# Low parts of the weights: a vector subtraction replaced by a second DMA that adds onto the negated rounded weights

## The chip, the cores and the metric

The kernel runs on one core of a Trainium2 chip. The metric is the device time of one execution in microseconds (us); three runs were made of the kernel before. Everything about where time goes comes from one execution taken by the hardware profiler.

## What is computed

Two transformer-like layers over 512 tokens of width 2048, in float32. The first (even) layer runs a gated depthwise convolution of 31 taps beside a block attention of 8 heads; the second (odd) layer runs a sparse latent attention of 16 heads whose keys are picked by an indexer. Cut to its products with weights:

```python
def _even_layer(x, ...):
    z = _rmsnorm(x, norm_g) @ w_in                       # 2048 x 7168
    ya = _conformer_conv(...) * silu(a_gate)             # holds a 1024 x 1024 product
    yb = _moba_attention(q, k, v) * silu(b_gate)
    return concatenate([ya, yb], -1) @ w_out             # 2048 x 2048

def _odd_layer(x, ...):
    z = _rmsnorm(x, norm_g) @ w_in                       # 2048 x 2896
    q = (_rmsnorm(cq, q_norm) @ w_qb)                    # then per head with w_uk, w_iq, w_uv
    return (o * silu(gate)) @ w_out                      # 2048 x 2048

x = x + _even_layer(x, ...)
x = x + _odd_layer(x, ...)
return _rmsnorm(x, final_norm)
```

## The kernel before

Activations lie with features on the 128 partitions and the 512 tokens along a row. Every float32 product is made of three products in the engine's rounded format fp32r: each operand is kept as a high part (rounded) and a low part (what is left), and `mm3` adds high by low (line 81), low by high (line 82) and high by high (line 83) into one PSUM tile.

Weights stream from DRAM in pieces of 128 rows by 512 columns (256 KB). `weights` handles one: SyncE's queue (SP) loads the piece into a raw tile `wr`, ScalarE rounds it into `wh` (line 90), VectorE subtracts `wh` from `wr` into `wl` (line 91, in `split`). One piece feeds four steps of a product over 2048 rows, so 12 matmuls. The tiles take turns in slots: `BUFS` gives `wr` four, `wh` and `wl` three each. `x` is split in the same way (lines 93 and 94).

`gemm` makes one output tile of 128 features by 512 tokens and calls `weights` for each piece. The first two tiles are made together by `gemm_pair`, which takes x as it arrives; there the pieces lie in tiles called `C` (raw), `T` (high) and `pt` (low), and the first pieces are smaller (128 and 384 columns). `final` makes the last three output tiles in halves of the tokens with twelve pieces that lie in `A` and `T`; behind that the output tiles take turns in the slots of `wr`, `wh` and `wl`.

The order on each engine comes from a scheduler that places instructions by priorities: `at(t)` sets the priority of what follows to a time t, and `weights` asks for its piece `LEAD` us ahead of the time at which it is wanted. Within an engine the order is then fixed, and an instruction that waits holds those behind it. POOL (GpSimd) does almost nothing.

The three lines that feed a piece:

```python
self.nc.sync.dma_start(raw[:, :n], dram)
i = nc.scalar.activation(th, src, AF.Copy)
nc.vector.tensor_tensor(tl, src, f32(th), op=OP.subtract)
```

Of the kernel before, what the change touches and what calls it, by code (L numbers as in the profile page):

```python
# [9 lines left out]
AF = mybir.ActivationFunctionType  # L10
OP = mybir.AluOpType
PSUM = bass.MemoryType.PSUM
# [3 lines left out]
T = 512  # L16
# [10 lines left out]
KTOP = 128  # L27
# [15 lines left out]
class Builder:  # L43
# [12 lines left out]

# [1 line left out]
    def at(self, t):  # L58
# [5 lines left out]

    BUFS = dict(A1=16, A2=16, G=8, Y=16, T=8, C=8, tmp=4, p=2, wr=4, wh=3, wl=3, u=2, pt=8, row=2, col=24, m8=6)

# [10 lines left out]

# [1 line left out]
    def mm3(self, ps, lh, ll, rh, rl, start, stop):  # L79
# [6 lines left out]
    def split(self, src, th, tl, scale=None):  # L86
        """th + tl = src (or src * scale, a column), th of 12 bits and tl what is left."""
        nc = self.nc
        if scale is None:
            i = nc.scalar.activation(th, src, AF.Copy)  # L90
            nc.vector.tensor_tensor(tl, src, f32(th), op=OP.subtract)  # L91
        else:
            i = nc.scalar.activation(th, src, AF.Copy, scale=scale)
            nc.vector.scalar_tensor_tensor(tl, src, scale, f32(th), op0=OP.mult, op1=OP.subtract)
        return getattr(i, "ins", i)

    LEAD = 8.0

    def weights(self, dram, t, tags=("wr", "wh", "wl")):
        """A piece [128, n] of a weight matrix as its two parts, wanted at t."""  # L100
        n = dram.shape[-1]
        self.at(t - self.LEAD)
        raw = self.s(tags[0], (P, PIECE))
        wh = self.s(tags[1], (P, PIECE), F32R)
        wl = self.s(tags[2], (P, PIECE), F32R)
        self.nc.sync.dma_start(raw[:, :n], dram)
        self.split(raw[:, :n], wh[:, :n], wl[:, :n])
        return wh, wl
# [3 lines left out]
    def gemm(self, dram, xs, m=P, tag="g", n=T):  # L112
        """PSUM tile [m, n] of dram.T @ x; dram is [128, kc, m] laid out flat, xs the parts of x."""
        nk = len(xs)
        ps = self.psum(tag)
        t0 = self.t
        per = PIECE // P
        cuts = list(range(0, nk, per)) + [nk]
        for k0, k1 in zip(cuts, cuts[1:]):
            nkk = k1 - k0  # L120
            wh, wl = self.weights(dram[:, k0 * m:(k0 + nkk) * m], t0 + self.STEP * k0)
            for k in range(nkk):
                self.at(t0 + self.STEP * (k0 + k))
                xh, xl = xs[k0 + k]
                i = self.mm3(ps[:m, :n], wh[:, k * m:(k + 1) * m], wl[:, k * m:(k + 1) * m], xh, xl,
                         k0 + k == 0, k0 + k == nk - 1)
                if k0 + k == 0:
                    self.marks.append((i.ins.name, t0))
        self.t = t0 + self.STEP * nk
        self.at(self.t)  # L130
        return ps
# [15 lines left out]

# [1 line left out]
    def colsum(self, src, rows=P, m=P):  # L149
# [4 lines left out]
    def inv_rms(self, dst, sq, n, rows=P, t=None, cs=range(NT), gap=1.0):  # L154
        """dst[p, t] = (sum_k sq[k, t] / n + EPS) ** -0.5 on every partition p, with one Newton step,
        for the row chunks cs; sq: the squares, or several to be added.  t: when its turn is, where it
        can wait.  Without dst it stays in the PSUM tile that is returned."""
        nc = self.nc
# [28 lines left out]

# [1 line left out]
    def attention(self, q, k, v, bias, ts, tt, tv, ptag="p"):  # L189
        """q (times -SCALE), k: parts [128 d, 512]; v(j): parts [128 s, 128 d]; bias(c): [128 t, 128 (c + 1)],  # L190
        0 or huge.  Returns PSUM [128 d, 512 t].  ts, tt, tv: when the logits, the transposes and the
        products with v have their turn on the tensor engine."""
        nc = self.nc
        # transposed probabilities: key block j holds rows 128 j .. 511; blocks 1 and 3 share a bank
        px = []
# [36 lines left out]

    # -----------------------------------------------------------------------
    def setup(self):
# [48 lines left out]
    def conv_in(self):  # L283
# [3 lines left out]
        for n in range(NCW):  # L287
            if n == 0:
                # the first two products share the pace at which x arrives
                pg, pv = self.gemm_pair(d["w_in"][NCW], d["w_in"][0])  # L290
                self.at(self.t)
            else:
                pg = self.gemm(d["w_in"][NCW + n], self.xs, tag="x" if n == 1 else "g")
# [63 lines left out]
    def even(self):  # L357
# [44 lines left out]
        for n in range(NCW):  # L402
# [5 lines left out]
            self.ys[n] = (yh, yl)  # L408
        # w_out's rows are laid out with those of the attention's half first
        ys = self.ys[NCW:] + self.ys[:NCW]  # L410
# [24 lines left out]
    def normed(self, zs, n, key, tag):  # L435
        """The parts of rmsnorm(z) * g for the tiles zs."""
        nc = self.nc
# [24 lines left out]
    def odd(self):  # L462
        nc, d = self.nc, self.d
        cq = self.normed([self.scaled(n, "C") for n in range(4)], 512, "q_norm", "G")
        ckv = self.normed([self.scaled(4 + n, "C") for n in range(2)], 256, "kv_norm", "T")
        # indexer keys and weights
        m = DI + HI
# [18 lines left out]
        nc.sync.dma_start(ik[DI:, :], ik[:DI, :])  # L486
        # parts of ik stacked for products of 128 rows: low over high and high over low
        lo, hi = slice(0, DI), slice(DI, P)
# [9 lines left out]
        nc.scalar.activation(zh[hi, :], ik[hi, :], AF.Copy)  # L498
        # gates fill the tensor engine while the indexer scores are formed
        gates = []  # L500
# [12 lines left out]
        for i in range(HI // 2):  # L513
            # the rows before KTOP keep all their keys and need no scores
            ps = self.gemm(d["w_iq"][i], [(a[:, KTOP:], b[:, KTOP:]) for a, b in cq], n=T - KTOP)
# [98 lines left out]
    def final(self):  # L614
        """The last product, with the final norm.  Its last tiles are done for the first half of the
        rows and then for the second, so that half of the output leaves under the second half."""
        nc, d = self.nc, self.d
# [5 lines left out]
        def take(n, x, ps, hs):  # L623
            """Columns hs of tile n are in ps."""
            nc.vector.tensor_tensor(x[:, hs], x[:, hs], ps, op=OP.add)  # L625
# [17 lines left out]
        for i in range(late):  # L643
            for k0 in range(0, KC, PIECE // P):
                n = KC - late + i
                ws.append(self.weights(d["w_out2"][n, :, k0 * P:k0 * P + PIECE],
                                       self.t + 5.2 * i + 0.325 * k0, ("wr",) + (("A2", "A2") if i < 2 else ("T", "T"))))
        # has the table of Sqrt at hand for the end
        warm = self.s("m8", (P, 8))
# [24 lines left out]

# bank and first column of each key block of the transposed probabilities
BLOCK = ((0, 0), (1, 0), (2, 0), (1, 384))
# [81 lines left out]
```

## Time and profile before

| | |
|---|---|
| median of 3 runs | 1553.35 us (1553.13 to 1553.88) |
| span of the profiled execution | 1552.0 us, first to last instruction; its own time is not listed apart from it |
| TensorE (PE) busy | 1531.0 us, 99% of the span |
| VectorE (DVE) busy | 987.0 us, 64% |
| ScalarE (ACT) busy | 658.1 us, 42% |
| GpSimd (POOL) busy | 0.4 us |
| DMA, mean share of 16 engines | 30.2%, 152.00 MB |
| granted TensorE clock, mean | 0.996 |

The median lies 1.35 us above the span. Busy time of TensorE counts overlapping products once; a product of 512 columns is listed with about 0.39 us and they start 0.229 us apart. A share of DMA is that of the time in which the 16 engines have packets; it can read slightly over 1 in a full stretch.

### The profile page before, as it was taken

The page shows a single profiled execution, that of the slowest core. Times are in us where ns is not written, and L with a number is a line of the kernel's source. Part 1 is how long each engine was busy: PE and PEld are TensorE (multiplying, and loading weights), DVE is VectorE, ACT ScalarE, POOL GpSimd, SP SyncE. Part 2 cuts the span into 40 slices and gives each one's busy share as a digit, 9 for nine tenths or more (in the row PEclk, how much of TensorE's full clock was granted, in tenths as well). Part 3 has the DMA queues.
Part 4 walks back from the last instruction along what each step waited for, and adds up shares of the span by engine and source line. Part 5 has one row for each costly group of instructions (what it writes and reads, how often), then busy time and mean ns, then how long its engine had stood idle before and what let it go on. Part 6 is the DMA issues. An engine that isn't in the chain of part 4 may idle for free.

```text
span 1552.0 us, 19982 instructions
## 1 busy us (share of the span) xinstructions
PE 1531.0 (99%) x7272; PEld 1276.3 (82%) x7272; DVE 987.0 (64%) x1933; ACT 658.1 (42%) x1177; POOL 0.4 (0%) x5
## 2 busy tenths in 40 slices
PE   8999999999999999999999999999999999999996
PEld 6888888888888888888888887788888888888886
DVE  7699999964654444464444444556598898843344
ACT  7433333334554343443333333445424666643341
POOL 0000000000000000000000000000000000000000
PEclk9999999999999999999999999999999999999998
DMA  6232222222222222224445332222232111133333
GB/s 222 88 102 96 95 96 95 95 86 83 83 83 88 82 88 86 86 86 136 146 140 150 118 99 80 84 89 89 82 96 88 55 51 53 55 122 116 124 128 109
DMA packets 86323, 153.28 MB, mean 99 GB/s; under 512 B 9488, under 2 KB 14736, under 8 KB 86224
## 3 DMA queue, kind: packets, MB, share of 16 engines
q1 hardware_dynamic: 86224, 152.00, 30.2%
q8 instruction: 57, 0.93, 0.3%
q14 instruction: 42, 0.34, 0.1%
HBM read 143.44 MB, written 8.39 MB: 98 GB/s over the span
## 4 chain that ended last, share of the span: by engine, by line
PE 98%; DVE 1%; ACT 0%; issue 0%; DMA 0%; SPq 0%; DVEq 0%; ACTq 0%
PE psg L81 29%; PE psg L83 29%; PE psg L82 29%; PE psx L215 2%; PE pss L82 1%; PE pss L81 1%; PE pss L83 1%; PE pso L82 1%; PE pso L83 1%; PE pso L81 1%; PE pss L528 0%; PE pss L529 0%; PE psx L83 0%; PE psx L82 0%; PE psx L81 0%; PE pso L182 0%
## 5 line engine op out<-in xcount | busy, mean ns | idle before, releaser
L90 ACT ACTIVATE wh<-wr 128x512 fp32r<-128x512 f32 (+1 forms) x480 | 302.1, 630 | 679.8 <-PE psg L83 556.5
L81 PE MATMUL psg<-A,wh 128*128 128x512 f32 x1472 | 580.6, 395 | 0.3 <-DVE tmp L625 0.2
L91 DVE TENSOR_TENSOR wl<-wr,wh 128x512 fp32r<-128x512 f32 (+1 forms) x480 | 330.7, 690 | 321.7 <-ACT wh L90 318.7
L83 PE MATMUL psg<-A,wh 128*128 128x512 f32 (+1 forms) x1264 | 496.3, 393 | 0.0
L82 PE MATMUL psg<-A,wl 128*128 128x512 f32 (+1 forms) x1264 | 495.6, 392 | 0.0
L81 PEld LDWEIGHTS psg<-A,wh 128*128 128x128 f32 x1472 | 276.0, 187 | 60.7 <-issue 1.5
L83 PEld LDWEIGHTS psg<-A,wh 128*128 128x128 f32 (+1 forms) x1264 | 236.8, 187 | 54.4 <-issue 1.2
L82 PEld LDWEIGHTS psg<-A,wl 128*128 128x128 f32 (+1 forms) x1264 | 236.8, 187 | 52.6 <-issue 1.4
L316 DVE SCALAR_TENSOR_TENSOR C<-u,cst,C 128x512 f32<-128x512 f32 x240 | 169.9, 750 | 0.2
L82 PE MATMUL psg<-Y,wl 128*128 128x512 f32 x336 | 131.7, 392 | 0.0
L83 PE MATMUL psg<-Y,wh 128*128 128x512 f32 x336 | 131.3, 391 | 0.0
L83 PE MATMUL psg<-G,wh 128*128 128x512 f32 (+1 forms) x224 | 85.9, 383 | 0.0
L82 PE MATMUL psg<-G,wl 128*128 128x512 f32 (+1 forms) x224 | 85.5, 382 | 0.0
L83 PEld LDWEIGHTS psg<-Y,wh 128*128 128x128 f32 x336 | 63.1, 188 | 14.1
L82 PEld LDWEIGHTS psg<-Y,wl 128*128 128x128 f32 x336 | 63.1, 188 | 13.1
L81 PE MATMUL psg<-T,wh 128*128 128x512 f32 x160 | 63.1, 394 | 1.1 <-DVE A L91 1.1
L81 PE MATMUL psg<-Y,wh 128*128 128x512 f32 x128 | 50.5, 394 | 0.0
L83 PEld LDWEIGHTS psg<-G,wh 128*128 128x128 f32 x224 | 42.0, 188 | 8.3
L82 PEld LDWEIGHTS psg<-G,wl 128*128 128x128 f32 x224 | 42.1, 188 | 7.7
L91 DVE TENSOR_TENSOR pt<-psx,pt 128x512 fp32r<-128x512 f32 (+1 forms) x72 | 42.2, 596 | 9.6 <-ACT pt L90 9.6
L90 ACT ACTIVATE pt<-psx 128x512 fp32r<-128x512 f32 (+1 forms) x72 | 35.7, 521 | 21.2 <-PE psx L215 21.0
L206 ACT ACTIVATE C<-C,col 128x128 f32<-128x128 f32 (+1 forms) x64 | 35.8, 560 | 15.6 <-DVE col L204 15.2
(231 smaller groups left out, 1781.1 us busy)
## 6 DMA issues: line engine op xcount, KB each, us to landing
wr<-in_w_in SPq DMA_DIRECT2D x304, 256.0 KB, 3.0
wr<-in_w_out SPq DMA_DIRECT2D x128, 256.0 KB, 3.0
wr<-in_w_qk SPq DMA_DIRECT2D x32, 256.0 KB, 2.5
Y<-in_xT SPq DMA_DIRECT2D x16, 256.0 KB, 6.1
wr<-in_w_pw SPq DMA_DIRECT2D x16, 256.0 KB, 2.8
tmp<-in_xT SPq DMA_DIRECT2D x16, 256.0 KB, 3.2
x<-tmp SPq DMA_DIRECT2D x16, 256.0 KB, 2.0
tmp<-x SPq DMA_DIRECT2D x16, 256.0 KB, 3.3
```

The source lines that it names most:

```text
L81: i = mm(ps, lh, rl, start=start, stop=False)
L82: mm(ps, ll, rh, start=False, stop=False)
L83: mm(ps, lh, rh, start=False, stop=stop)
L90: i = nc.scalar.activation(th, src, AF.Copy)
L91: nc.vector.tensor_tensor(tl, src, f32(th), op=OP.subtract)
L206: nc.scalar.activation(p[:, :w], p[:, :w], AF.Exp, bias=mn, scale=-1.0, accum_out=sm)
L215: nc.tensor.transpose(px[b][:, o:o + P], p[:, j * P:(j + 1) * P], self.ident)
L316: nc.vector.scalar_tensor_tensor(y, u[:, i:i + T], self.c("w_dw", n * TAPS + i), y, op0=OP.mult, op1=OP.add)
```

## The change

In `weights` the low part is no longer made by VectorE. ScalarE copies the raw piece twice, once rounded into `wh` and once rounded and negated into `wl`, and a second DMA of the same piece from DRAM, issued from POOL's queue, adds the weights onto `wl` (weights minus rounded weights). The slots go from four to two for `wr` and from three to four for `wh` and `wl`, and `LEAD` from 8 to 11. `split` itself stays for activations. Comment lines fall away.

```diff
-    BUFS = dict(A1=16, A2=16, G=8, Y=16, T=8, C=8, tmp=4, p=2, wr=4, wh=3, wl=3, u=2, pt=8, row=2, col=24, m8=6)
+    BUFS = dict(A1=16, A2=16, G=8, Y=16, T=8, C=8, tmp=4, p=2, wr=2, wh=4, wl=4, u=2, pt=8, row=2, col=24, m8=6)
...
-    LEAD = 8.0
+    LEAD = 11.0
...
         self.nc.sync.dma_start(raw[:, :n], dram)
-        self.split(raw[:, :n], wh[:, :n], wl[:, :n])
+
+        self.nc.scalar.activation(wh[:, :n], raw[:, :n], AF.Copy)
+        self.nc.scalar.activation(wl[:, :n], raw[:, :n], AF.Copy, scale=-1.0)
+        self.nc.gpsimd.dma_start(wl[:, :n], dram, accum_op=OP.add)
         return wh, wl
```

ScalarE at the start of the program, before the change. `Y` is a column block of x as loaded, `A` its parts; `C` are raw pieces of weights and `T` their high parts:

```order
L93 ACTIVATE A_4_80<-Y_78,xg 128x512
L90 ACTIVATE T_245<-C_244 128x128
L90 ACTIVATE T_251<-C_250 128x128
L93 ACTIVATE A_7_86<-Y_84,xg 128x512
L90 ACTIVATE T_263<-C_262 128x384
L90 ACTIVATE T_269<-C_268 128x384
L93 ACTIVATE A_10_92<-Y_90,xg 128x512
L93 ACTIVATE A_13_98<-Y_96,xg 128x512
L90 ACTIVATE T_293<-C_292 128x512
L93 ACTIVATE A_16_104<-Y_102,xg 128x512
```

The same place after the change, where lines 108 and 109 are the two copies and `pt` takes the negated one:

```order
L108 ACTIVATE T_245<-C_244 128x128
L109 ACTIVATE pt_246<-C_244 128x128
L108 ACTIVATE T_252<-C_251 128x128
L109 ACTIVATE pt_253<-C_251 128x128
L93 ACTIVATE A_4_80<-Y_78,xg 128x512
L108 ACTIVATE T_265<-C_264 128x384
L109 ACTIVATE pt_266<-C_264 128x384
L108 ACTIVATE T_272<-C_271 128x384
L109 ACTIVATE pt_273<-C_271 128x384
L93 ACTIVATE A_7_86<-Y_84,xg 128x512
L108 ACTIVATE T_297<-C_296 128x512
L109 ACTIVATE pt_298<-C_296 128x512
```

Each piece now takes two places in ScalarE's queue, and both pieces of a pair stand ahead of the next block of x.

TensorE in the last part of the pair, before the change: `psg` and `pss` are the two output tiles of the pair, `A_41` to `A_50` the low parts of the last four blocks of x, and behind them begins the next tile, `psx`:

```order
L81 MATMUL psg_242<-A_47_165,T_365 128x512
L82 MATMUL psg_242<-A_46_164,pt_366 128x512
L83 MATMUL psg_242<-A_46_164,T_365 128x512
L81 MATMUL pss_243<-A_47_165,T_371 128x512
L82 MATMUL pss_243<-A_46_164,pt_372 128x512
L83 MATMUL pss_243<-A_46_164,T_371 128x512
L81 MATMUL psg_242<-A_50_171,T_365 128x512
L82 MATMUL psg_242<-A_49_170,pt_366 128x512
L83 MATMUL psg_242<-A_49_170,T_365 128x512
L81 MATMUL pss_243<-A_50_171,T_371 128x512
```

The same place after the change:

```order
L81 MATMUL psg_242<-A_50_171,T_373 128x512
L82 MATMUL psg_242<-A_49_170,pt_374 128x512
L83 MATMUL psg_242<-A_49_170,T_373 128x512
L82 MATMUL pss_243<-A_40_152,pt_381 128x512
L83 MATMUL pss_243<-A_40_152,T_380 128x512
L81 MATMUL pss_243<-A_44_159,T_380 128x512
L82 MATMUL pss_243<-A_43_158,pt_381 128x512
L83 MATMUL pss_243<-A_43_158,T_380 128x512
L81 MATMUL pss_243<-A_47_165,T_380 128x512
L82 MATMUL pss_243<-A_46_164,pt_381 128x512
L83 MATMUL pss_243<-A_46_164,T_380 128x512
L81 MATMUL pss_243<-A_50_171,T_380 128x512
```

The two tiles no longer alternate by block of x: four blocks go into `psg`, then the same four into `pss`. From the first product with the 13th block (`A_41`) up to where `psx` has TensorE for itself there are 36 products, one of them of `psx`; from the first with the last block (`A_50`) there are 14.

ScalarE beside the softmax of an attention head of the even layer (line 206 before, 209 after, is the exponential), before the change:

```order
L90 ACTIVATE wh_2675<-wr_2674 128x512
L90 ACTIVATE wh_2693<-wr_2692 128x512
L206 ACT_TABLE_LOAD
L206 ACTIVATE p_2596,col_2598<-p_2596,col_2597 128x128
L206 ACTIVATE p_2611,col_2613<-p_2611,col_2612 128x256
L90 ACTIVATE wh_2711<-wr_2710 128x512
```

The same head after the change:

```order
L109 ACTIVATE wl_2805<-wr_2803 128x512
L108 ACTIVATE wh_2804<-wr_2803 128x512
L209 ACT_TABLE_LOAD
L209 ACTIVATE p_2706,col_2708<-p_2706,col_2707 128x128
L209 ACTIVATE p_2721,col_2723<-p_2721,col_2722 128x256
L109 ACTIVATE wl_2824<-wr_2822 128x512
L108 ACTIVATE wh_2823<-wr_2822 128x512
```

The table load and the two exponentials stand between two pieces as before; the negated copy stands ahead of the rounded one.

## Rows read from the trace of the kernel before

**Rows 1.** Page, span and part 1: busy us (share of the span) xinstructions.
```profile
span 1552.0 us, 19982 instructions
PE 1531.0 (99%) x7272; PEld 1276.3 (82%) x7272; DVE 987.0 (64%) x1933; ACT 658.1 (42%) x1177; POOL 0.4 (0%) x5
```

**Rows 2.** Page, the chain that ended last, by engine.
```profile
PE 98%; DVE 1%; ACT 0%; issue 0%; DMA 0%; SPq 0%; DVEq 0%; ACTq 0%
```

**Rows 3.** Busy time by stretch: us, engines, PEclk, DMA share, GB/s.
```profile
39.00:1536.00 1497.00, 1495.22 (x7122) 1247.61 (x7121) 950.60 (x1861) 628.26 (x1126) 0.00 (x0) 1.00 0.30 95
```

**Rows 4.** What TensorE waited for: us in total, times, longest.
```profile
PE psg L81 <- DVE A L94: 6.8, 1, 6.8
```

**Rows 5.** Page, costliest groups: busy us, mean ns, idle before and its releaser.
```profile
L90 ACT ACTIVATE wh<-wr 128x512 fp32r<-128x512 f32 (+1 forms) x480 | 302.1, 630 | 679.8 <-PE psg L83 556.5
...
L91 DVE TENSOR_TENSOR wl<-wr,wh 128x512 fp32r<-128x512 f32 (+1 forms) x480 | 330.7, 690 | 321.7 <-ACT wh L90 318.7
...
L206 ACT ACTIVATE C<-C,col 128x128 f32<-128x128 f32 (+1 forms) x64 | 35.8, 560 | 15.6 <-DVE col L204 15.2
```

**Rows 6.** Timeline of one piece: start us, us, engine, line.
```profile
299.66 0.39 PE L83 MATMUL psg<-A,wh 128*128 128x512 f32 x1
...
301.17 0.33 SPq L106 DMA_DIRECT2D wr<-in_w_in  x1
...
302.41 0.39 PE L83 MATMUL psg<-A,wh 128*128 128x512 f32 x1
```

**Rows 7.** DMA from 100 to 300 us: queue share; issues, KB, us to landing.
```profile
q1 hardware_dynamic: 10444, 19.02, 28.7%
...
wr<-in_w_in SPq DMA_DIRECT2D x73, 256.0 KB, 3.0
```

**Rows 8.** The same from 700 to 870 us, the even layer's output product.
```profile
q1 hardware_dynamic: 13070, 23.79, 46.0%
...
wr<-in_w_out SPq DMA_DIRECT2D x62, 256.0 KB, 3.2
```

**Rows 9.** The same from 0 to 25 us.
```profile
Y<-in_xT SPq DMA_DIRECT2D x16, 256.0 KB, 6.1
```

**Rows 10.** Busy time by stretch of the start; last two: DMA share, GB/s.
```profile
10.00:12.00 2.00, 2.00 (x8) 1.63 (x8) 1.71 (x3) 1.99 (x4) 0.00 (x0) 1.00 1.05 394
...
22.00:24.00 2.00, 2.00 (x10) 1.63 (x10) 1.56 (x3) 1.60 (x4) 0.00 (x0) 1.00 1.07 406
```

**Rows 11.** Timeline of ScalarE at the start.
```profile
3.84 1.28 ACT L93 ACT_TABLE_LOAD   x1 [3.84 <-DMA xg<-in_xg]
5.13 0.72 ACT L93 ACTIVATE A<-Y,xg 128x512 fp32r<-128x512 f32 x1
5.76 0.49 ACT L90 ACTIVATE T<-C 128x128 fp32r<-128x128 f32 x2
...
9.33 0.52 ACT L90 ACTIVATE T<-C 128x384 fp32r<-128x384 f32 x1 [1.84 <-DMA C<-in_w_in]
...
13.20 2.02 ACT L93 ACTIVATE A<-Y,xg 128x512 fp32r<-128x512 f32 x3
...
23.35 1.37 ACT L93 ACTIVATE A<-Y,xg 128x512 fp32r<-128x512 f32 x2 [0.40 <-DMA Y<-in_xT]
```

**Rows 12.** Timeline of the start: TensorE, VectorE, and ScalarE behind the pair.
```profile
7.77 0.63 PE L82 MATMUL psg<-A,pt 128*128 128x512 f32 x1
...
12.69 0.75 DVE L94 SCALAR_TENSOR_TENSOR A<-Y,xg,A 128x512 fp32r<-128x512 f32 x1
...
27.23 1.66 ACT L90 ACTIVATE wh<-wr 128x512 fp32r<-128x512 f32 x3
...
30.99 0.39 PE L81 MATMUL psx<-A,wh 128*128 128x512 f32 x1
```

**Rows 13.** The end: one output tile on VectorE; landing of the stores.
```profile
1542.31 0.75 DVE L671 TENSOR_TENSOR wr<-G,pso 128x256 f32<-128x256 f32 x2 [1.38 <-PE pso L182]
...
outT<-wr SPq DMA_DIRECT2D x6, 256.0 KB, 2.8
```

## The prediction

> **What bounds the kernel now.** I read the page's busy shares first, then the chain that ended last, then what TensorE waited for, and then two stretches closely: the start and an ordinary stretch in the middle. The reader should see one engine only. TensorE is busy 1531.0 of 1552.0 us [rows 1], the chain is TensorE for 98% [rows 2], and of the 1497 us between 39 and 1536 us it is idle for 1.8 [rows 3]. What is left outside lies at the two ends: TensorE's only long wait, 6.8 us before the first product [rows 4], and the last 10 us, in which the output tiles are scaled and stored [rows 13]. VectorE, whose subtraction the change takes away, is busy 64% and ScalarE 42%, and neither holds TensorE anywhere in the middle. So a subtraction that goes can give nothing back there; what matters is whether the new way of making a low part is ever late.
>
> How late it may be is read from the slots. A piece of weights feeds 12 products, and the products stand 2.75 us apart per piece (299.66 to 302.41) [rows 6]. ScalarE's rounding of a piece waits for TensorE to give a slot back (556.5 of the 679.8 us that it idles ahead of those instructions) [rows 5]: it runs as early as the slots let it, and the rest of the chain behind it has time to spare.
>
> **The change part by part.** *Removed:* 480 subtractions of 690 ns from VectorE, 331 us [rows 5], and 22 more like them in the first pair of products and the last three. They lay beside TensorE's work; worth 0 on the path.
>
> *Added on ScalarE:* 502 negated copies. One of 128x512 takes 630 ns as the rounding does [rows 5], so some 310 us: ScalarE goes from 658 to about 970 us, 62% of the span. In the middle that is 1.26 of each 2.75 us, beside TensorE; cost 0 unless something else queues behind it (below).
>
> *Added DMAs:* 502 more transfers of up to 256 KB, behind the negated copy, from POOL's queue. The trace of before has no accumulating transfer and none from POOL. Bounds of its landing: not less than a plain load of the same piece, 3.0 us [rows 7], and for the upper end 6.1 us, what a load takes when the engines are full [rows 9]. An accumulating piece also reads SBUF; the nearest row is the plain load, so I take 3.0 plus the 0.8 us for which a piece holds the engines (28.7% of 2.75 us [rows 7]) = 3.8 us, and keep 3.0 and 6.1. With four slots a piece comes round every 11.0 us; TensorE holds it 2.75, ScalarE needs 1.26, so the transfer may take 7.0 us. Both ends fit. Where an attention head's work stands in ScalarE's queue ahead of a weight piece (a table load of 1.28 us [rows 11] and two exponentials of 0.56 [rows 5] at the place that the order shows), 4.6 us are left: 3.8 fits, 6.1 is 1.5 us late. Over 24 heads that is 0 to 36 us; I take 0.2 a head, an estimate, 5 us.
>
> The Trainium skill ("DMA: Bandwidth & Descriptors", Anatomy of one DMA) gives a transfer issued from GpSimd 2.0 us plus its bytes at 436 GB/s, so an estimate of 2.6 us for a piece. The rows have 3.0 us for a piece from SP's queue, and no run here yet shows one from POOL's. By the page the steady part would cost 0, too.
>
> *Moved: the raw slots.* They go from four to two, and a raw slot is given back only after both copies. Its loop is the landing, two copies (1.26) and SP's issue (0.33 [rows 6]); two slots allow 5.5 us, so the landing may take 3.9 us. It takes 3.0 [rows 7], and 3.2 in the stretch of the output product, where a load and a store of x lie beside [rows 8]. The negated copy that frees the slot also starts the accumulating transfer, so the two now meet on the engines. The lower bound is 3.0; the upper 4.6 is 3.0 plus twice 0.8, if the accumulating piece counts double and lies wholly ahead. At 4.6 a piece comes each 3.1 us instead of 2.75: 0.35 x 440 = 150 us. The nearest row is the stretch with other transfers beside, 3.2, which is hidden: 0, and 150 kept as the upper end.
>
> *Moved: the start.* Here three chains run side by side, and each slips.
> ScalarE: the order shows both copies of two pieces ahead of each few columns of x. Up to the split of the 13th column it now has a table load that ends at 5.1 us, 13 splits at 0.72 (9.4), four copies of 0.25, four of 0.52 and twelve of 0.63 (10.6 instead of 5.3) [rows 11]: 25.1 us, with VectorE's part of 0.75 25.9. From there TensorE's order has 36 products to go at 0.229 (2.75 / 12): the first product behind the pair stands at 34.1 us instead of 30.99 [rows 12], +3. Where copies overlap, as three did in 1.66 us [rows 12] and three splits in 2.02 [rows 11], the chain is 1.9 us shorter: +1.
> The DMA engines: from 10 to 24 us they are full, at about 0.38 MB/us [rows 10]. Eight of the ten accumulating pieces, 1.6 MB, come ahead of the last x: 4.1 us, or 8.3 if each counts double. The last x was split from 23.35 on [rows 11]; behind it must come 0.72, 0.75 and 14 products (3.2), so 2.9 us of the 7.6 up to 30.99 are spare: +1 to +5.
> The first low part: ready at 5.6 us (table load, two copies) plus a landing of 3.0 to 6.1, 8.6 to 11.7, where TensorE took its third product at 7.77 [rows 12]: +1 to +4. Products of that first stretch are listed with 0.63 us where later ones have 0.39 [rows 12], though the granted clock is shown as 1.00, the upper level; that stretch will come later as a whole.
> If they lay wholly side by side the slip would be the largest of them, 1 to 5; if the first two followed on the third, up to 9. I take +5. Then ScalarE squares x between the next pieces, whose accumulated parts have no lead yet: +2, an estimate (a landing of 3.8 against a lead of some 2 us, once).
>
> *The end.* The output tiles take turns in `wr`, `wh`, `wl`; with two `wr` the third waits for the first's store, which lands 2.8 us after its issue, and it comes six tiles of up to 0.75 behind the first, some 4 us [rows 13]: 0, at most 1.
>
> **Sum.** 1552.0 + 5 + 2 (start) + 5 (heads) + 0 (raw loop) + 0 (end) = 1564 us of span. The profile lists the span alone for its execution; the median of the runs is 1.35 above it, so 1565.4. I say **1566 us**.
>
> **The rivals.**
> 1. *The raw loop binds at times* (landing between 3.9 and 4.6 us). For it: two slots, and both transfers start at the same copy. Against: 3.2 us where other transfers lie beside. Up to 1566 + 150; I take half, 1640.
> 2. *An accumulating packet costs the engines twice a plain one.* The plain pieces take 28.7% of the engines [rows 7], the accumulating ones 57%; together 86% in the ordinary stretches, and 46.0 + 57 = 103% in the output product [rows 8], which is past full. There a landing of 6.1 us gives a piece each (6.1 + 1.59) / 2 = 3.85 us, +1.1 over 128 pieces = 141; elsewhere a landing half way between 3.0 and 6.1 gives 3.07, +0.32 over 300 pieces = 96. That is 1566 + 237 = 1803 us. For it: it reads two operands for each one written; against: no row shows that reading is the engine's limit. The Trainium skill ("Collectives: The Full Stack", The bandwidth ceiling) states it as the rule: an adding transfer has two source reads on the same ring and runs at half the rate of a copy, 32.35 against 62.28 GB/s. No run here shows it so far.
> 3. *Not slower.* The start's work fits into what is idle there. The mechanism: ScalarE's copies overlap (0.55 each) and the accumulating transfers queue behind the loads of x, whose last is still split at 23 us. Then the ScalarE chain gives +1, the first low part +1, and the rest 0: 1554 to 1556. It decides when the slip of the first product behind the pair is under 3 us. For it: the 2.9 us to spare behind the last x; against: both engines would have to be without a pause from 4 us on.
> 4. *Faster.* VectorE, freed of 331 us, would have to end the waits in the middle; those come to 1.8 us [rows 3], so at best 1551.5, and only with no loss at the start.
>
> **How the numbers follow.** The forecast (start slips, the rest is hidden but for small stalls; own range 1557 to 1585) 0.50; rival 1, 0.22; rival 2, 0.15; rival 3, 0.10; rival 4, 0.03. The measurement tells about 0.2%, 3.1 us, from no change. Slower by more than that: 0.50 + 0.22 + 0.15 = 0.87; within 0.10; faster 0.03. The range reaches from 1555, which takes half of rival 3, to 1720, the upper end of rival 1: 0.50 + 0.22 + 0.05, and the lower part of rival 2, about 0.8.
>
> **What would show it.** Right: 502 transfers in POOL's queue landing in 3 to 5 us, VectorE's busy time down by some 335 us and ScalarE's up by some 310; the first product into `psx` at 34 to 38 us; TensorE idle below 10 us from 45 to 1536 us. The raw loop: landings of `wr` over 3.9 us, and TensorE waiting at line 81 for ScalarE's `wh`. The double price: DMA shares near 0.85 in the ordinary stretches, TensorE waiting at line 82 for `wl`. The prediction is wrong if the accumulating transfer lands later than 7 us in steady state, since then every piece waits for it; or if TensorE, broken by many short waits, is granted less clock, which no stretch of before shows.

## The result and the profile after

The changed kernel takes 1643.9 us (median of four runs, 1638.24 to 1646.28) where the kernel before, on the same chip, takes 1553.62 (1553.13 to 1554.69): a ratio of 1.0575, 95% interval 1.0558 to 1.0591, so 90 us slower. The profiled execution is the quickest of its four, 1638.24 us with a span of 1636.5, 84.5 more than the span of [rows 1]; the ledger below is made in spans.

The page of the changed kernel: span, busy times, the chain that ended last, the two DMA queues (q0 is POOL's, q1 is SP's; packets, MB, share of 16 engines), and the issues of weights (KB each, us to landing).

```profile
span 1636.5 us, 21088 instructions
...
PE 1564.8 (96%) x7272; PEld 1274.6 (78%) x7272; DVE 677.9 (41%) x1431; ACT 906.0 (55%) x1679; POOL 435.6 (27%) x507
...
q0 software_dynamic: 72288, 130.71, 45.9%
q1 hardware_dynamic: 86224, 152.00, 33.8%
...
issue 43%; PE 30%; POOL 16%; DMA 7%; ACT 2%; DVE 1%; SPq 0%; POOLq 0%; ACTq 0%; DVEq 0%
...
wr<-in_w_in SPq DMA_DIRECT2D x304, 256.0 KB, 4.0
wl<-in_w_in POOLq DMA_DIRECT2D x304, 256.0 KB, 5.2
wr<-in_w_out SPq DMA_DIRECT2D x128, 256.0 KB, 4.7
wl<-in_w_out POOLq DMA_DIRECT2D x116, 256.0 KB, 5.8
```

VectorE lost 309 us of work and ScalarE gained 248, as the change asks. TensorE has the same 7272 products, but it no longer makes up the chain: 30% of it instead of 98 [rows 2]. A plain load of a piece, 3.0 to 3.2 us before [rows 7, 8], now lands in 4.0 to 4.7, and the accumulating transfers take 5.2 to 5.8.

The waits of the changed kernel (engine, tile and line, what it waited for: us in total, times, longest):

```profile
ACT wl L109 <- DMA wr<-in_w_in: 242.4, 147, 3.8
ACT wl L109 <- DMA wr<-in_w_out: 160.5, 90, 5.1
ACT wl L109 <- PE psg L82: 158.5, 126, 4.2
```

Before, ScalarE's first operation on a piece waited for TensorE to give a slot back (556.5 us, [rows 5]); now it waits in 237 cases for the raw piece itself. That is the sign of a raw loop that is too short. Beside it, TensorE's own waits look small:

```profile
PE psg L82 <- DMA wl<-in_w_out: 23.3, 19, 3.8
...
PE psg L82 <- DMA wl<-in_w_in: 5.1, 13, 0.7
...
PE psx L81 <- ACT wh L108: 3.5, 1, 3.5
```

The first two name the accumulated part, the last link of the chain, not the link that is short. Whoever reads only this view would blame the accumulating transfer alone; it is what lengthens the landings (run 2), but with more raw slots it costs little (run 5). The view also shows only a part of the loss. TensorE's idle time grew from 21.0 to 71.7 us (span less busy time), and its listed busy time from 1531.0 to 1564.8 us for the same 7272 products, together the 84.5 us. The weight loads of line 82 wait 65.0 us for `wl` (38.4 for `w_out` and 26.6 for `w_in`) where the products wait 28.4: a gap of a few tenths of a microsecond vanishes under products listed with 0.39 us. A lower granted clock adds some, see below.

Where the 84.5 us lie is read from four lines of VectorE that run once per output tile: the convolution's gate, a tile of each attention head of the even layer, and the two residual additions. Of before (times are the start of the first and of the last):

```profile
L303 DVE SCALAR_TENSOR_TENSOR u<-tmp,cst,tmp x8: 717/747/749, 58.2 to 265.6; 128x512 f32<-128x512 f32 x8
L368 DVE SCALAR_TENSOR_TENSOR tmp<-psg,r x8: 680/692/693, 285.7 to 633.9; 128x512 f32<-128x512 f32 x8
L419 DVE TENSOR_TENSOR tmp<-tmp,psg x16: 686/686/686, 727.3 to 892.3; 128x512 f32<-128x512 f32 x16
L625 DVE TENSOR_TENSOR tmp<-tmp,psg x19: 420/687/689, 1380.0 to 1537.4; 128x512 f32<-128x512 f32 x13, 128x256 f32<-128x256 f32 x6
```

The same four of the changed kernel, whose lines stand three further down:

```profile
L306 DVE SCALAR_TENSOR_TENSOR u<-tmp,cst,tmp x8: 718/750/753, 72.1 to 290.1; 128x512 f32<-128x512 f32 x8
L371 DVE SCALAR_TENSOR_TENSOR tmp<-psg,r x8: 679/692/693, 312.7 to 662.1; 128x512 f32<-128x512 f32 x8
L422 DVE TENSOR_TENSOR tmp<-tmp,psg x16: 686/690/692, 755.6 to 950.5; 128x512 f32<-128x512 f32 x16
L628 DVE TENSOR_TENSOR tmp<-tmp,psg x19: 410/687/690, 1446.6 to 1621.6; 128x512 f32<-128x512 f32 x13, 128x256 f32<-128x256 f32 x6
```

The differences of neighbouring marks make a ledger by stage; the same marks were read in every experiment (us of the profiled execution; the loss is against before):

| stage | before | changed | loss | four raw slots | three raw slots, in order |
|---|---|---|---|---|---|
| start, to the first gate | 58.2 | 72.1 | 13.9 | 73.1 | 68.8 |
| convolution, to the first L368 | 227.5 | 240.6 | 13.1 | 229.2 | 229.1 |
| even attention, to the first L419 | 441.6 | 442.9 | 1.3 | 442.0 | 444.1 |
| output product 1, L419 first to last | 165.0 | 194.9 | 29.9 | 166.3 | 170.4 |
| odd layer, to the first L625 | 487.7 | 496.1 | 8.4 | 488.3 | 488.2 |
| output product 2, L625 first to last | 157.4 | 175.0 | 17.6 | 164.3 | 166.2 |
| end | 14.6 | 14.9 | 0.3 | 15.0 | 14.7 |
| span | 1552.0 | 1636.5 | 84.5 | 1578.2 | 1581.5 |

The loss is largest where pieces of weights follow each other with nothing between them, the output products and the convolution, and is nearly nothing in the even attention, where other products stand between (145 pieces in 442.9 us, 3.05 us a piece).

What goes on there shows between 100 and 300 us, first in the DMA view:

```profile
q0 software_dynamic: 9858, 17.97, 50.4%
q1 hardware_dynamic: 9849, 17.92, 35.2%
...
wl<-in_w_in POOLq DMA_DIRECT2D x69, 256.0 KB, 5.4
wr<-in_w_in SPq DMA_DIRECT2D x69, 256.0 KB, 4.9
```

69 pieces in 200 us are 2.90 us a piece, where before 73 came, 2.74 [rows 7]. And in ScalarE's timeline of that stretch (start us, us, engine, line; in brackets the idle time before and what ended it):

```profile
206.11 0.63 ACT L109 ACTIVATE wl<-wr 128x512 fp32r<-128x512 f32 x1 [0.69 <-DMA wr<-in_w_in]
206.65 0.62 ACT L108 ACTIVATE wh<-wr 128x512 fp32r<-128x512 f32 x1
...
208.93 0.63 ACT L109 ACTIVATE wl<-wr 128x512 fp32r<-128x512 f32 x1 [1.66 <-DMA wr<-in_w_in]
```

ScalarE is idle ahead of most pieces (56 waits for raw pieces, 87.9 us in all, between 100 and 300 us) and starts them when the raw piece lands. Read so, the loop of the two raw slots sets the pace; runs 5 and 9 test it.

### The profile page after: what moved, and what is told of

Read it like the earlier page. It is cut to its first block, busy times and chain, and to the rows that moved or that the text cites. A ratio compares the mean times of both kernels' runs of the same rounds, so it can differ in the third digit from the quotient of the medians.

```text
span 1636.5 us, 21088 instructions
## 1 busy us (share of the span) xinstructions
PE 1564.8 (96%) x7272; PEld 1274.6 (78%) x7272; DVE 677.9 (41%) x1431; ACT 906.0 (55%) x1679; POOL 435.6 (27%) x507
## 3 DMA queue, kind: packets, MB, share of 16 engines
q0 software_dynamic: 72288, 130.71, 45.9%
q1 hardware_dynamic: 86224, 152.00, 33.8%
## 4 chain that ended last, share of the span: by engine, by line
issue 43%; PE 30%; POOL 16%; DMA 7%; ACT 2%; DVE 1%; SPq 0%; POOLq 0%; ACTq 0%; DVEq 0%
POOL wl L110 16%; PE psg L81 8%; PE psg L82 8%; PE psg L83 8%; DMA wr<-in_w_out 4%; PE psx L218 1%; ACT wh L108 1%; DMA wr<-in_w_in 1%; PE pss L82 1%; PE pso L82 1%; PE pso L83 1%; PE pss L83 1%; PE pss L81 1%; DMA C<-in_w_in 1%; PE pso L81 1%
## 5 line engine op out<-in xcount | busy, mean ns | idle before, releaser
L109 ACT ACTIVATE wl<-wr 128x512 fp32r<-128x512 f32 (+1 forms) x480 | 302.0, 629 | 609.9 <-DMA wr<-in_w_in 242.4
L82 PE MATMUL psg<-A,wl 128*128 128x512 f32 (+1 forms) x1264 | 502.5, 398 | 5.8 <-DMA wl<-in_w_in 5.1
L110 POOL DMA_DIRECT2D wl<-in_w_in x304 | 263.5, 867 | 666.8 <-ACT wl L109 646.9
L82 PEld LDWEIGHTS psg<-A,wl 128*128 128x128 f32 (+1 forms) x1264 | 236.8, 187 | 77.3 <-DMA wl<-in_w_in 26.6
L108 ACT ACTIVATE wh<-wr 128x512 fp32r<-128x512 f32 (+1 forms) x480 | 295.1, 615 | 2.3 <-DMA wr<-in_w_in 1.3
L319 DVE SCALAR_TENSOR_TENSOR C<-u,cst,C 128x512 f32<-128x512 f32 x240 | 175.5, 750 | 5.7
L110 POOL DMA_DIRECT2D wl<-in_w_out x116 | 100.4, 866 | 276.2 <-ACT wl L109 265.1
L83 PE MATMUL psg<-Y,wh 128*128 128x512 f32 x336 | 131.8, 392 | 0.0
L82 PEld LDWEIGHTS psg<-G,wl 128*128 128x128 f32 x224 | 42.7, 191 | 34.0 <-DMA wl<-in_w_out 26.6
L422 DVE TENSOR_TENSOR tmp<-tmp,psg 128x512 f32<-128x512 f32 x16 | 11.0, 689 | 124.9 <-PE psg L83 124.9
L110 POOL DMA_DIRECT2D wl<-in_w_qk x32 | 27.7, 866 | 120.2 <-ACT wl L109 112.8
```

The source lines that it names most:

```text
L82: mm(ps, ll, rh, start=False, stop=False)
L83: mm(ps, lh, rh, start=False, stop=stop)
L108: self.nc.scalar.activation(wh[:, :n], raw[:, :n], AF.Copy)
L109: self.nc.scalar.activation(wl[:, :n], raw[:, :n], AF.Copy, scale=-1.0)
L110: self.nc.gpsimd.dma_start(wl[:, :n], dram, accum_op=OP.add)
L319: nc.vector.scalar_tensor_tensor(y, u[:, i:i + T], self.c("w_dw", n * TAPS + i), y, op0=OP.mult, op1=OP.add)
```

## The experiments

Ten kernels ran, each timed beside the kernel before on the same chip. The stage times of a run come from its one profiled execution. The diffs are against the changed kernel where nothing else is said. Two theories stood against each other: **A**, the loop of two raw slots is too short for the landings that the second transfer makes longer; **B**, the DMA engines are as good as full (45.9 + 33.8 = 79.7% of the span, 50.4 + 35.2 = 85.6% in the stretch above), and no number of slots helps. Each expectation words them anew for its run.

**Run 1 (e1). Three raw slots (inconclusive).** So that the tiles take no more memory, `wh` gives one up.

```diff
-    BUFS = dict(..., wr=2, wh=4, wl=4, ..., pt=8, ...)
+    BUFS = dict(..., wr=3, wh=3, wl=4, ..., pt=8, ...)
```

> The changed kernel with three raw slots, three for the high parts and four for the low ones (wr 3, wh 3, wl 4 instead of 2, 4, 4). Theory A (the raw loop is the bound: the accumulating transfers push the landing of a raw piece from 3.0 to 4.0 to 5.1 us, over the 3.9 that two slots allow): three slots allow 6.7 us, so the losses of the convolution stretch (13 us) and most of that of the two output products (30 and 18 us) go; 1585 to 1605 us. Theory B (the engines or the landing of the accumulating piece itself are the bound, whatever the slots): 1630 to 1650 us.

Measured: 1640.8 us, 1.0544 (1.0507 to 1.0581). That is what B asks for. But the edit did something else too. The order of ScalarE's instructions, in which `wr` numbers name the raw piece:

```
L109 ACTIVATE wl_1555<-wr_1553 128x512
L108 ACTIVATE wh_1535<-wr_1534 128x512
L109 ACTIVATE wl_1574<-wr_1572 128x512
L108 ACTIVATE wh_1554<-wr_1553 128x512
```

With three `wh` the rounding of a piece stands behind the negation of the next one, so the third raw slot is held until the next piece lands, and is as good as absent: ScalarE still waits 277.7 and 150.1 us for raw pieces of `w_in` and `w_out`. The run can't tell the theories apart; run 9 repeats it without this.

**Run 2 (e2). A plain second load.** The transfer from POOL's queue only copies; the low part then holds the whole weight, which changes the sum but not the work on any other engine.

```diff
-        self.nc.gpsimd.dma_start(wl[:, :n], dram, accum_op=OP.add)
+        self.nc.gpsimd.dma_start(wl[:, :n], dram)
```

> The changed kernel with the second transfer as a plain copy from POOL's queue instead of an addition: same count, bytes from DRAM, queue and waits, but the destination is not read. The low part then holds the whole weight and not what is left of it. Theory A with the price of the addition (an accumulating packet holds the engines longer because it reads twice): POOL's queue falls from 45.9% of the engines to some 30%, a raw piece lands in 3.3 to 3.7 us, 1570 to 1595 us. If it is the second transfer as such (its queue, its issue, a second read of DRAM) and not the addition: 1630 to 1645 us.

Measured: 1587.82 us, 1.0219 (1.0192 to 1.0245), inside the range of A. The landing of a raw piece, expected at 3.3 to 3.7 us, was missed: it stays at 4.0 to 4.3. The page of this kernel:

```profile
q1 hardware_dynamic: 86224, 152.00, 30.6%
q0 software_dynamic: 72288, 130.71, 30.1%
...
wr<-in_w_in SPq DMA_DIRECT2D x304, 256.0 KB, 4.0
wl<-in_w_in POOLq DMA_DIRECT2D x304, 256.0 KB, 4.1
wr<-in_w_out SPq DMA_DIRECT2D x128, 256.0 KB, 4.3
wl<-in_w_out POOLq DMA_DIRECT2D x116, 256.0 KB, 4.4
```

The same bytes on the same queue hold the engines 30.1% instead of 45.9%; per MB that is 3.65 us of all 16 engines (0.301 x 1586.0 / 130.71) against 5.75 (0.459 x 1636.5 / 130.71), 1.57 times. With four raw slots the same comparison gives 1.48 times (48.8% of 1578.2 us in run 5, 33.3% of 1561.0 in run 6). Against the plain loads of before, 3.08 (0.302 x 1552.0 / 152.00), it is 1.86 times. How much of this is two streams in each other's way is not taken apart. So most of the 84.5 us, 50.5 (1636.5 less 1586.0), comes with the adding, and 32 with a second transfer of any kind beside the first (1586.0 less the 1554.0 of run 3).

**Run 3 (e3). No second transfer.** The line of the second DMA is taken out; the low part is then only the negated high one.

```diff
-        self.nc.gpsimd.dma_start(wl[:, :n], dram, accum_op=OP.add)
```

> The changed kernel without the second transfer: both copies stay on ScalarE, the low part stays the negated rounded weight. Theories A and B alike: raw landing back at 3.0 us, the middle and both output products without loss, only the start 1 to 4 us later; 1553 to 1560 us. If ScalarE's doubled copies or the slots are what costs: 1590 us or more.

Measured: 1556.12 us, 1.0010 (1.0001 to 1.0019); span 1554.0, start 60.4, convolution 227.0, output products 165.0 and 157.3. ScalarE's 502 extra copies, the two raw slots and the new order together cost 2 us of span. ScalarE is not the bound, and two raw slots are enough as long as landings stay at 3.0 us.

**Run 4 (e4). Slots and lead alone.** The kernel before with the numbers of the change and the subtraction kept; against the kernel before:

```diff
-    BUFS = dict(..., wr=4, wh=3, wl=3, ...)
+    BUFS = dict(..., wr=2, wh=4, wl=4, ...)
-    LEAD = 8.0
+    LEAD = 11.0
```

> The kernel before (subtraction on VectorE) with the slots and the lead of the changed one: wr 2, wh 4, wl 4, LEAD 11. Theory A and B: a raw piece lands in 3.0 us, under the 3.9 that two slots allow, so within 3 us of the kernel before, 1551 to 1557 us. If two raw slots cost without any accumulating transfer: 1570 us or more.

Measured: 1554.93 us, 1.0001 (0.9992 to 1.0011). The change of slots does harm only together with the second transfer.

**Run 5 (e5). Four raw slots.** Now all three tags keep four, and `pt` gives up two.

```diff
-    BUFS = dict(..., wr=2, wh=4, wl=4, ..., pt=8, ...)
+    BUFS = dict(..., wr=4, wh=4, wl=4, ..., pt=6, ...)
```

> The changed kernel with four raw slots (wr 4, wh 4, wl 4; pt goes from 8 to 6 to make room). In the run with three raw slots and three for the high parts, a rounding stands behind the negation of the next piece in ScalarE's queue, so a raw slot was held one piece longer and that run did not free the loop. Theory A (the raw loop of two slots with landings of 4 to 5 us): four slots allow 9.4 us, so the convolution stretch loses nothing (228 us instead of 241) and the output products lose less; 1595 to 1615 us. Theory B (the engines are full, or the landing of the accumulating piece is the bound, whatever the raw slots): the first shows DMA shares near 0.9 as before, and 1630 to 1645 us.

Measured: 1574.75 us, 1.0140 (1.0124 to 1.0157): 69 us of the 90 are gone, with every accumulating transfer still there. That is 20 us below the range of A, which left the output products a loss that they don't have. ScalarE's longest wait in this kernel:

```profile
ACT wl L109 <- PE psg L82: 526.1, 384, 4.2
```

The two waits of its negation for a raw piece, 242.4 and 160.5 us in the changed kernel, are down to 0.6 us together, and the wait for TensorE is back at 526.1 us, near the 556.5 of [rows 5]. The convolution's stretch is 229.2 us and the first output product 166.3, nearly those of before. The busy times of 100 to 300 us in this kernel, the last three columns being the granted clock, the DMA share and GB/s:

```profile
100.00:300.00 200.00, 200.00 (x874) 163.86 (x873) 169.52 (x243) 106.02 (x170) 62.69 (x73) 1.00 0.95 192
```

and its landings over the whole span:

```profile
wr<-in_w_in SPq DMA_DIRECT2D x304, 256.0 KB, 5.2
wl<-in_w_in POOLq DMA_DIRECT2D x304, 256.0 KB, 5.8
```

TensorE is busy for all of the 200 us while the DMA engines are at 0.95, fuller than in the changed kernel (0.86), and pieces land later than there (5.2 and 5.8 us). Theory B falls: with slots enough, neither near-full engines nor landings of nearly 6 us cost anything in this stretch.

**Run 6 (e6). Four raw slots and a plain second load.** Runs 2 and 5 together.

> The same four raw slots with the second transfer as a plain copy (destination not read; the low part then holds the whole weight). Theory A: the plain second load is hidden when the raw loop is free, leaving the start and little else, 1563 to 1574 us. Theory B: as with two raw slots, 1584 to 1592 us.

Measured: 1561.77 us, 1.0050 (1.0035 to 1.0065), a little under what A gave. Convolution 227.0, output products 164.7 and 158.1: with plain loads four raw slots hide everything behind the start, which ends at 66.7.

**Run 7 (e7). The start subtracted.** The first pair's ten pieces (their raw tiles are `C`) are made by VectorE as before.

```diff
+        if tags[0] == "C":
+            self.split(raw[:, :n], wh[:, :n], wl[:, :n])
+            return wh, wl
```

> The changed kernel, but the ten pieces of the first pair of products make their low parts by subtraction on VectorE as before; all others by the accumulating transfer. If the start's loss (13.9 us up to the first gated tile) comes from those ten transfers and their copies: that tile at 59 to 63 us instead of 72.1, and 1630 to 1637 us. If it comes from what follows: 1641 us or more.

Measured: 1629.95 us, 1.0489 (1.0468 to 1.0509), at the lower edge of the first range; the start ends at 62.6 instead of 72.1, the other stages are within 5 us of the changed kernel's. Ten of 502 transfers, with their copies, carry 9.5 of the 13.9 us that the start loses.

**Run 8 (e8). The start and both output products subtracted.** The same, and the pieces of both `w_out`.

```diff
+        if tags[0] == "C" or dram.tensor.name in ("in_w_out", "in_w_out2"):
```

> Low parts by subtraction in the first pair and in both output products (138 pieces), by the accumulating transfer in the other 364. What is left of the loss is that of the convolution stretch (13 us) and of the stretches between (some 9): 1572 to 1584 us on either theory; the output products at the pace of before (165 and 157 us) with two raw slots. If they keep a loss, two raw slots and not the accumulating transfers beside x cost there.

Measured: 1581.96 us, 1.0181 (1.0163 to 1.0198). The output products are back at 165.0 and 157.6 us with two raw slots, at landings of 3.1 us in the DMA view of 760 to 900 us:

```profile
wr<-in_w_out SPq DMA_DIRECT2D x50, 256.0 KB, 3.1
```

The convolution, where pieces still come by the adding transfer, keeps its 241.6. So each stage pays for its own transfers, and the stages add up.

**Run 9 (e10). Three raw slots, in order.** Run 1 again with four `wh`; the negation and the rounding of a piece stand next to each other again.

```diff
-    BUFS = dict(..., wr=2, wh=4, wl=4, ..., pt=8, ...)
+    BUFS = dict(..., wr=3, wh=4, wl=4, ..., pt=7, ...)
```

> Three raw slots as in e1, but four rounded and four low ones, so that ScalarE's queue keeps the order of the changed kernel (negation, then rounding, of the same piece). Three slots let a raw landing take up to about 6.7 us before the loop is longer than a piece's 2.75 us; the changed kernel's landings are 4.0 to 5.1. Theory A (the loop of two raw slots carried the loss, and e1 failed only because its order held a slot one piece longer): about the time of the kernel with four raw slots, 1574 to 1585 us, the convolution's stretch near 230 us instead of 240.6. Theory B (three slots don't help, whatever the order; the engines' share is what counts): 1630 to 1645 us, the stretch near 241.

Measured: 1584.9 us, 1.0195 (1.0173 to 1.0217), at the upper edge of what A gave. The convolution takes 229.1 us as with four. The waits of this kernel:

```profile
ACT wl L109 <- PE psg L82: 484.7, 353, 4.2
...
ACT wl L109 <- DMA wr<-in_w_out: 47.9, 20, 4.2
```

A third slot cures the convolution; in the output products, where x and its stores take turns with the weights, 20 waits for raw pieces stay, and those stages take 4.1 and 1.9 us more than with four. The 56 us between runs 1 and 9 differ by one `wh` slot, one `pt` slot and the order on ScalarE that they bring.

**Run 10 (e11). Four raw slots, and the subtraction for the first pair and the last twelve pieces.** 480 pieces still come by the adding transfer.

```diff
-    BUFS = dict(..., wr=2, wh=4, wl=4, ..., pt=8, ...)
+    BUFS = dict(..., wr=4, wh=4, wl=4, ..., pt=6, ...)
+        if tags[1] != "wh":
+            self.split(raw[:, :n], wh[:, :n], wl[:, :n])
+            return wh, wl
```

> Four raw, rounded and low slots, and the pieces of the start and the last twelve made by the subtraction as before; 480 pieces still come by the adding transfer. Theory A (the ledger adds up: what four raw slots leave over is the start's ten pieces and the last output product): the start near 62.6 us instead of 73, the second output product near 158 instead of 164, the whole 1556 to 1564 us. Theory B (the remainder of 21 us comes from the adding transfers as such, wherever they stand): 1570 us or more.

Measured: 1562.36 us, 1.0054 (1.0038 to 1.0069), within what A gave for the whole; the start ends at 61.3. The second output product, though, takes 162.4 us, not the 158 expected. Most of its loss of 5.0 us sits at one place, in TensorE's timeline:

```profile
1506.48 0.28 PE L81 MATMUL psg<-A,A 128*128 128x256 f32 x1
1509.20 0.50 PE L82 MATMUL psg<-Y,wl 128*128 128x512 f32 x1 [2.44 <-DMA wl<-in_w_out]
...
1510.88 0.63 PE L82 MATMUL psg<-Y,wl 128*128 128x512 f32 x1
```

and in the busy times of the stretch around it:

```profile
1480.00:1500.00 20.00, 20.00 (x89) 16.43 (x88) 2.07 (x3) 9.15 (x16) 5.72 (x7) 1.00 0.95 215
1500.00:1520.00 20.00, 17.56 (x98) 15.29 (x97) 10.49 (x16) 9.83 (x18) 0.86 (x1) 0.91 0.54 152
```

TensorE waits 2.44 us for one accumulated piece, and over the 20 us the granted clock is 0.91 on average: the products listed with 0.63 us are those at the lower level, 1.2 GHz. ScalarE's timeline shows why the piece is late (the subtracted pieces lie in `A`):

```profile
1496.31 0.62 ACT L112 ACTIVATE wl<-wr 128x512 fp32r<-128x512 f32 x1
...
1499.42 0.63 ACT L90 ACTIVATE A<-wr 128x512 fp32r<-128x512 f32 x1 [1.98 <-DMA wr<-in_w_out]
1502.33 0.63 ACT L90 ACTIVATE A<-wr 128x512 fp32r<-128x512 f32 x1 [2.28 <-DMA wr<-in_w_out]
1502.87 0.61 ACT L112 ACTIVATE wl<-wr 128x512 fp32r<-128x512 f32 x1
```

Its negation stands behind the roundings of two of the last twelve pieces, ahead of each of which ScalarE idles about 2 us until the raw piece lands. So it starts 6.56 us after the negation before it instead of some 2.75, and POOL issues the transfer at 1503.78; the landing itself, some 5.4 us up to 1509.2, is an ordinary one. No run tests another order there.

## Why the prediction was right in its direction and wrong in its size

The forecast was 1566 us, the result 1643.9, which is rival 1's 1640 and inside the range. By the prediction's own steps, against the spans of the ledger:

- *The subtractions removed, 0.* Right: VectorE's 309 us gave nothing back; run 3, which has lost them as well, is 2 us longer than before.
- *ScalarE's copies, 0 in the middle.* Right, and for the reason given: 906.0 us busy instead of the 970 forecast, since copies in a row overlap (two in 1.16 us, 206.11 to 207.27, not 1.26), and run 3 shows the stages at their old lengths.
- *The accumulating transfer, 3.8 us (3.0 to 6.1).* Mis-sized, and by itself nearly harmless: 5.2 to 5.8 us, near the upper bound, and run 5 hides 5.8 us under the 7.0 that four slots allow. The Trainium skill's 2.0 us plus bytes at 436 GB/s ("DMA: Bandwidth & Descriptors", Anatomy of one DMA) would give an estimate of 2.6 us; the traces do not agree with it here, since even the plain copy from POOL's queue takes 4.1 to 4.4 beside the raw loads (run 2).
- *The heads, +5.* The even attention lost 1.3 us. The odd layer's 8.4 are not the heads' queueing: with four raw slots 0.6 of them stay.
- *The raw slots, "hidden: 0".* **This is the step that failed.** The limit was worked out rightly: two slots let a piece land in 3.9 us, and 4.6 was named as the price if the accumulating piece counts double. I took 3.2 ("The nearest row is the stretch with other transfers beside"), though the transfers of that row are plain ones and take 46.0% of the engines. The runs showed 4.9 us in the convolution and 4.7 as the median of the output weights, beyond even the upper end. By the prediction's formula 4.9 gives (4.9 + 1.26 + 0.33) / 2 = 3.25 us a piece; the trace has 2.90. The overlap of the two copies (1.16) brings the formula to 3.20; the rest is not taken apart. The sum of the middle stages, 13.1 + 1.3 + 29.9 + 8.4 + 17.6 = 70.3 us, stands where the prediction has 0 and 5; four raw slots take 59.4 of it away (10.9 stay: 1.7 + 0.4 + 1.3 + 0.6 + 6.9). Of the two signs named for the raw loop the first came, landings over 3.9 us. The second did not: no wait of line 81 for `wh` stands in the middle; TensorE waits at line 82 for `wl`, which was named as the sign of the double price. The `wl` of a piece is ready one transfer (5.2 to 5.8 us) after its negation, its `wh` 1.16 us after the negation starts, so a raw piece that is late is felt at line 82.
- *The start, +7.* Right in kind, half of the size: 13.9. The runs take it apart, from one execution each: slots and lead 1.9 (run 4, 60.1), ScalarE's copies 0.3 more (run 3, 60.4), a second transfer of the plain kind 5.1 (run 2, 65.5), the adding 6.6 (72.1). ScalarE's chain, first of the three in the prediction, is the cheapest of them; the bytes ahead of the last x are the dear ones. They delay x itself (a block lands in 8.6 us instead of 6.1, [rows 9]), and a new wait follows from it, below.
- *The end, 0.* Right: 0.3.

The rivals: rival 1 is what happened. That its 1640 lies so near 1643.9 is in part luck: it is half of an upper end, taken without a row, and beside it the start was 7 us too small and the heads some 4 too large. Rival 2 was near the price and had the consequence wrong. Its 86% for the ordinary stretches is the 0.86 that the trace shows between 100 and 300 us, but by luck: the accumulating pieces take 50.4% instead of 57, the plain ones 35.2 instead of 28.7. The Trainium skill's half rate for an adding transfer ("Collectives: The Full Stack", The bandwidth ceiling), which the prediction set beside it, is stated there of a reduce-scatter against an all-gather. The traces here stay under that factor of two: 1.57 on the same queue, 1.86 against undisturbed loads. The full engines make the landings longer; what made these costly was the loop of two slots, as run 5 shows at a share of 0.95. The two rivals were one chain: the price of rival 2 brings about the landing of rival 1. Had I carried the doubled piece, for which I gave 0.15, into the raw loop instead of keeping it as a case apart, the forecast would have been rival 1's.

The start has one more link, which the prediction named only as a way to be wrong. TensorE's timeline of the changed kernel, near the end of the first pair:

```profile
30.09 0.40 PE L81 MATMUL psg<-A,T 128*128 128x512 f32 x1
33.94 0.79 PE L81 MATMUL psx<-A,wh 128*128 128x512 f32 x1 [3.45 <-ACT wh L108]
34.53 0.63 PE L82 MATMUL pss<-A,pt 128*128 128x512 f32 x1
```

and the busy times there, clock, DMA share and GB/s last:

```profile
30.00:32.00 2.00, 0.49 (x3) 0.10 (x1) 0.55 (x2) 0.72 (x1) 0.00 (x0) 1.00 1.11 262
32.00:34.00 2.00, 0.06 (x1) 0.06 (x1) 0.72 (x1) 0.74 (x2) 0.00 (x0) 0.72 0.94 277
34.00:36.00 2.00, 2.00 (x5) 1.61 (x6) 0.75 (x1) 2.00 (x5) 0.86 (x1) 0.50 0.21 66
```

The one product of `psx` that the order puts among those of the pair (36 with it, as the prediction counted) waits 3.45 us for a raw piece that lands late, and the pair's products wait behind it. After that idle stretch the granted clock is 0.50, the lower level of 1.2 GHz, and twelve products from 34.53 to 39.65 us stand 0.43 apart instead of 0.229: 2.4 us more. The output products show it three times more, behind waits of 1.84 us (to 827.90), 3.78 (to 844.53) and 2.43 (to 1578.29): the granted clock is 0.54, 0.50 and 0.50 in stretches of 2 us that follow. Two other waits, 1.74 us (to 788.54) and 1.98 (to 920.93), were not followed by it. From the clock of those stretches each of the three cost some 1.7 us, an estimate, so about 7.5 of the 84.5 us are clock: a term that the prediction's sum lacks.

What stays open: the 10.9 us of the middle stages with four raw slots. Of the 6.9 in the second output product, run 5's trace has 4.7 as waits for accumulated pieces, and some 1.7, an estimate, as the lower clock behind one of them; in run 10 one late piece and the clock behind it are about 4 of 5.0. The other 4.0 us are not taken apart. No run beat the kernel before; TensorE is busy for 99% of it, so what a moved subtraction could give back is at most the 1.8 us of waits in [rows 3].

## What to carry to other kernels

Work out for each ring of buffers how long a transfer may take (slots times the time per piece, less what else holds a slot), and then put into it the landing that the change itself brings about, not the one of the trace before: a second stream of transfers lengthens the first one's landings, and the ring with the least room pays, even if it belongs to the stream that was not touched. A wait names the last link; which ring is short is seen one engine upstream, where a wait for a slot has turned into a wait for data. A run with more slots tells a short ring from full engines, but the order on each engine must stay the same, or the slot that was added is held by something else.

## What the hardware showed unexpectedly

- An accumulating DMA from DRAM into SBUF holds the DMA engines 1.57 times as long per MB as a plain one on the same queue (1.48 with four raw slots), and the plain loads beside it take longer too: 0.352 x 200 / 69 = 1.02 us of the 16 engines for a piece, against 0.287 x 200 / 73 = 0.79 before [rows 7].
- POOL is occupied by an issue: 435.6 us in all with accumulation and 265.6 with plain copies, over 502 transfers about 0.87 and 0.53 us each. It was never near full (27% and 17% of the span), but the issue is a link of a late piece's chain: 16% of the chain that ended last in the changed kernel.
- DMA engines busy to 0.95 over 200 us cost TensorE nothing when the rings were long enough (run 5).
- Single idle stretches of TensorE were followed by a lower granted clock: four times in the changed kernel (behind 3.45, 1.84, 3.78 and 2.43 us) and once in the second output product of run 10 (behind 2.44 us; 0.91 on average over 1500 to 1520 us). The first cost 2.4 us more, that of run 10, as an estimate from 0.09 x 20, 1.8.
